# 28 of 48 modulation blocks computed on ScalarE and GpSimd instead of TensorE, in a two-layer diffusion backbone

## The chip, the cores and the metric

The kernel runs on one core of one Trainium2 chip. The metric is the device time of one execution in microseconds (us), the median over several runs. Engines are named as the profile names them: PE is TensorE, ACT is ScalarE, DVE is VectorE, POOL is GpSimd, SP is the engine that issues the DMAs.

## The reference, cut to what matters

Two layers over 256 latent and 256 context tokens of width 1024. Each layer turns a conditioning vector (`c` for latent tokens, `c_ctx` for context tokens) into six modulation vectors of 1024 numbers: shift, scale and gate of the mixer, and the same of the feed-forward.

```python
mod  = jax.nn.silu(c)     @ w_mod[l] + b_mod[l]      # w_mod[l]: 1024 x 6144
modc = jax.nn.silu(c_ctx) @ w_mod[l] + b_mod[l]
sh1, sc1, gt1, sh2, sc2, gt2 = jnp.split(mod[:, None, :], 6, axis=-1)
h = rms_norm(xl, g_pre_mix[l]) * (1.0 + sc1) + sh1
y, yc = token_mixer(h, hc, ...)          # conv branch, attention, pooling, merged by gates
xl = xl + gt1 * rms_norm(y, g_post_mix[l])
h = rms_norm(xl, g_pre_ffn[l]) * (1.0 + sc2) + sh2
xl = xl + gt2 * rms_norm(swiglu(h, ...), g_post_ffn[l])
```

The context tokens do the same with `modc`, in the first layer only (their second layer is never read).

## The kernel before

All products are float32, made of three passes of rounded floats: `split` (L345) writes `hi` on ACT (L347) and the rest `lo` on DVE (L348), and `mm3` (L328) multiplies hi·hi, hi·lo and lo·hi. Weights come in units of 128x1024, one DMA each, in the fixed order of `weight_order`; `unit` (L309) keeps about five units prepared ahead. A scheduler that goes by a simulated timeline then orders each engine's instructions and may move them past each other; on the chip each engine works its own list strictly in that order.

A layer (`layer`, L915) goes: V projection; eight heads, each with q and k projection (evicted at L606, one shuffled product on POOL at L611), scores, softmax (L704 to L716), transposes and the product with V (`head`, L719); in the first layer then the GLU projection (`glu`, L778) and the pooling projection, whose window sums run on POOL (`pool_group`, L876, L893 to L908); the depthwise convolution as 120 taps on DVE (L824) with a norm after it; `subln` (L748), which normalises the heads' outputs four heads at a time; three rounds of eight `merge` steps (attention, pooling, conv branch, in this order; L977); the output projection; the feed-forward's 22 pairs of units (L1089) and its output projection. The second layer does GLU and taps first.

The modulation is made in **blocks** of 256 columns: 24 per layer, four to each of the six vectors (`j` = 0 to 5; 2 and 5 are the gates). `mod_product` (L373) multiplies a block on PE: eight plain-float32 matmuls with 32 columns of `silu(c)` (`self.cc`, of which two are not zero), four chunks of the 1024 side by side in four strips of 32 rows. `mod_close` (L387) ends a block. For a shift or a scale ACT copies the strips out (L416), PE transposes them (L422, two), DVE adds the four strips, the bias and so on into `modv`. For a gate ACT and DVE split the strips, and PE spreads them over all partitions for each vector (`v`: latent, context) with two matmuls (L400, L401); DVE adds the bias and multiplies the norm's gain (L410, L412) into `G`, the tile that `residual` reads.

Eight blocks are made at the very start (shift and scale of layer 0's mixer). The others lie along the way: the mixer gate in the heads (L954), shift and scale of the feed-forward in the last merge round (`new_modv_fill`, L1106), four blocks at the end of the output projection `wo` (three in the second layer) and three at the end of `fo`, where PE would otherwise wait for the norm (L557, L585), and the rest beside the feed-forward's pairs (L1095). `BUFS` (L220) says how many buffers each kind of tile has: `mod` (a block's weights) has 2, `V` 18.

Of the kernel before, what the change touches and what calls it, by code (L numbers as in the profile page):

```python
# [30 lines left out]
DEPTH = 2  # L33
# [15 lines left out]
COL_G = 4608  # L49
UW = 1024  # L50


O_BM = 0
O_GM = 48
O_GF = 56
# [140 lines left out]
def lay_mod(w):  # L196

    m = w["w_mod"].reshape(DEPTH, 2, 4, P, 24, 256)
    return np.ascontiguousarray(m.transpose(0, 4, 1, 3, 2, 5)).reshape(
        DEPTH * 48, P, UW)  # L200


class Net:
    def __init__(self, ctx, tc, io):
# [14 lines left out]

    BUFS = {"raw": 4, "hi": 4, "lo": 4, "rawx": 4, "hix": 2, "lox": 3, "mod": 2, "H": 4, "V": 18, "O": 8, "Q": 10,  # L220
            "E": 7, "A": 6, "T": 4, "S": 2, "G": 4, "row": 2, "rows": 3, "sq": 4, "K2": 2, "QD": 1, "QH": 2, "QL": 2, "st": 25, "sh": 1,
# [165 lines left out]
    def mod_close(self, l, b, ps, gate=None):  # L387
# [46 lines left out]
        if j in (1, 4):  # L434
            nc.vector.scalar_tensor_tensor(out=d, in0=d, scalar=1.0,
                                           in1=col(O_GM if j == 1 else O_GF),
                                           op0=ALU.add, op1=ALU.mult)

    def new_modv(self, l):
# [103 lines left out]
    def out_proj(self, l, kind, nkp, acts, ntt, x, jg, tail, last, fill=()):  # L543
# [233 lines left out]

    def glu(self, l, acts, n, after_first):  # L778

        nc = self.nc  # L780
        us = []
        for i in range(NCC):
# [132 lines left out]
    def layer(self, l, H, acts, first, xin, xnext, tail):  # L915
# [12 lines left out]
        if not need_ctx:  # L928
            us = self.glu(l, acts, n, None)
            taps, norm = self.conv_tasks(l, us, nseq, ya)  # L930
            self.bg.extend(taps)
# [4 lines left out]
        pend = None  # L936
        self.new_G(l, 2)
        fill = deque(range(8, 12))
        for h in range(NH):
# [14 lines left out]
            if h % 2 == 0 and fill:  # L954
                self.mod_block(l, fill.popleft(), bank=self.H_BK)
        os.append(self.head(l, *pend, lam, need_ctx))

        if need_ctx:
            us = self.glu(l, acts, n, None)
            taps, norm = self.conv_tasks(l, us, nseq, ya)  # L960
        else:
            self.drain()
# [42 lines left out]
        for n_ in range(KC):  # L1005
            merge(1, n_, yb, ("ao", l, n_), 0)
            self.step(self.S_B)

# [19 lines left out]
        x = self.load_x(xin, ntt, "Q")  # L1028
        self.new_modv_fill(l)
        for n_ in range(KC):  # L1030
            merge(0, n_, ya, ("co", l, n_ // 2) if n_ % 2 == 0 else None,
                  (n_ % 2) * 4)
            if self.fill:
                self.fill.popleft()()
            if n_ >= 4 and self.fill:
                self.fill.popleft()()
        while self.fill:
            self.fill.popleft()()

# [49 lines left out]
        for i in range(i0, NFF):  # L1089
# [5 lines left out]
            if fill:  # L1095
                self.mod_block(*fill.popleft(), bank=self.FF_BK)
        while fill:
# [8 lines left out]
    def new_modv_fill(self, l):  # L1106

        self.fill = deque()
        for part in range(4):
            for j in (3, 4):  # L1110
                if l > 0 and (part, j) in ((0, 3), (0, 4), (1, 3)):
                    continue
                self.fill.append(lambda b=j * 4 + part: self.mod_block(l, b, bank=self.FL_BK))

# [10 lines left out]
    def run(self):  # L1125
        nc, io = self.nc, self.io
        self.prm, self.modv, self.G = {}, {}, {}
        self.perm = self.sb.tile([P, NPERM], F32, tag="perm", name="perm", bufs=1)
        const = self.perm[:, 0:C_TAB]
# [10 lines left out]
        self.ones512 = const[:, C_ONE:C_ONE + 1].to_broadcast([P, P])  # L1140
        perm_r = self.sb.tile([P, 6], F32R, tag="permr", name="perm_r", bufs=1)
# [4 lines left out]
        self.eps = self.perm[:, M_EPS:M_EPS + 1]  # L1146
        nc.vector.memset(self.eps, EPS)
        self.cc = (self.perm[:, M_CC:M_CC + 32 * KC]
# [130 lines left out]
```

## Time and profile before

| | |
|---|---|
| median of 3 runs | 1562.87 us (1561.74 to 1565.12) |
| the profiled execution | 1560.56 us, its span 1558.8 us |
| busy share of the span: PE, DVE, ACT, POOL | 98%, 63%, 48%, 9% |
| granted TensorE clock, mean | 0.995 of 2.4 GHz |
| DMA: moved, mean rate | 236.69 MB, 152 GB/s |

An engine's share is an average over stages. Matmuls are pipelined: in the records of a row of them each starts about 0.23 us (512 columns) or 0.12 us (256 columns) after the one before, though each is shown as lasting longer. So the cost of a matmul is read from start to start.

### The profile page before, as it was taken

The page shows a single profiled execution, that of the slowest core. Times are in us where ns is not written, and L with a number is a line of the kernel's source. Part 1 is how long each engine was busy: PE and PEld are TensorE (multiplying, and loading weights), DVE is VectorE, ACT ScalarE, POOL GpSimd, SP SyncE. Part 2 cuts the span into 40 slices and gives each one's busy share as a digit, 9 for nine tenths or more (in the row PEclk, how much of TensorE's full clock was granted, in tenths as well). Part 3 has the DMA queues.
Part 4 walks back from the last instruction along what each step waited for, and adds up shares of the span by engine and source line. Part 5 has one row for each costly group of instructions (what it writes and reads, how often), then busy time and mean ns, then how long its engine had stood idle before and what let it go on. Part 6 is the DMA issues. An engine that isn't in the chain of part 4 may idle for free.

```text
span 1558.8 us, 22462 instructions
## 1 busy us (share of the span) xinstructions
PE 1521.7 (98%) x8616; PEld 1254.0 (80%) x8616; DVE 979.8 (63%) x1626; ACT 740.6 (48%) x1254; POOL 144.5 (9%) x170
## 2 busy tenths in 40 slices
PE   6999999999999999999999999999998999999998
PEld 3778878878777688877888888888787799799986
DVE  4588786899964337434333222899999665665544
ACT  5467767432344236322222221836576565554443
POOL 0000100640131100000000000001012312100000
PEclk9999999999999999999999999999999999999999
DMA  9643343133335544456322234534344674546553
GB/s 347 200 121 95 108 136 95 69 117 100 128 111 193 201 143 149 145 169 202 102 95 95 95 122 162 201 126 135 107 133 146 245 257 167 208 157 206 185 191 108
DMA packets 81691, 236.69 MB, mean 152 GB/s; under 512 B 9648, under 2 KB 18480, under 8 KB 81584
## 3 DMA queue, kind: packets, MB, share of 16 engines
q1 hardware_dynamic: 81584, 235.26, 46.1%
q8 instruction: 67, 1.10, 0.3%
q14 instruction: 40, 0.33, 0.1%
HBM read 223.69 MB, written 5.24 MB: 147 GB/s over the span
## 4 chain that ended last, share of the span: by engine, by line
PE 89%; DVE 5%; ACT 2%; DMA 1%; issue 1%; POOL 1%; SPq 0%; DVEq 0%; ACTq 0%; POOLq 0%
PE psg L332 15%; PE psg L331 15%; PE psg L333 15%; PE pss L331 10%; PE pss L333 10%; PE pss L332 9%; PE pso L332 3%; PE pso L331 3%; PE pso L333 3%; PE pss L701 2%; PE pss L380 2%; PE pst L380 1%; PE pst L732 1%; DVE Q L824 1%; DVE lo L348 1%
## 5 line engine op out<-in xcount | busy, mean ns | idle before, releaser
L347 ACT ACTIVATE hi<-raw 128x1024 fp32r<-128x1024 f32 x299 | 314.7, 1055 | 523.0 <-issue 155.0
L348 DVE TENSOR_TENSOR lo<-raw,hi 128x1024 fp32r<-128x1024 f32 x299 | 373.3, 1250 | 278.3 <-ACT hi L347 273.7
L331 PE MATMUL psg<-H,hi 128*128 128x512 f32 (+1 forms) x864 | 299.8, 348 | 2.6 <-ACT E L707 1.5
L332 PE MATMUL psg<-H,hi 128*128 128x512 f32 (+1 forms) x864 | 299.2, 347 | 0.7 <-DVE H L348 0.7
L333 PE MATMUL psg<-H,lo 128*128 128x512 f32 (+1 forms) x864 | 299.7, 347 | 0.0
L331 PE MATMUL pss<-H,hi 128*128 128x256 f32 (+1 forms) x704 | 236.6, 337 | 1.8 <-ACT H L347 1.7
L333 PE MATMUL pss<-H,lo 128*128 128x256 f32 (+1 forms) x704 | 235.4, 335 | 0.0
L332 PE MATMUL pss<-H,hi 128*128 128x256 f32 (+1 forms) x704 | 234.4, 333 | 0.2 <-DVE H L348 0.2
L331 PEld LDWEIGHTS psg<-H,hi 128*128 128x128 f32 x864 | 162.1, 188 | 29.6 <-issue 3.2
L332 PEld LDWEIGHTS psg<-H,hi 128*128 128x128 f32 x864 | 162.3, 188 | 24.5 <-issue 3.4
L333 PEld LDWEIGHTS psg<-H,lo 128*128 128x128 f32 x864 | 162.4, 188 | 22.5 <-issue 2.2
L331 PEld LDWEIGHTS pss<-H,hi 128*128 128x128 f32 x704 | 132.5, 189 | 18.9 <-issue 2.5
L332 PEld LDWEIGHTS pss<-H,hi 128*128 128x128 f32 x704 | 133.8, 190 | 14.3 <-DVE H L348 0.4
L333 PEld LDWEIGHTS pss<-H,lo 128*128 128x128 f32 x704 | 132.6, 188 | 14.9
L611 POOL TENSOR_TENSOR sh<-sh,perm 128x256 f32<-128x256 f32 x32 | 27.8, 868 | 817.8 <-DMA raw<-w 494.2
L824 DVE SCALAR_TENSOR_TENSOR Q<-Q,perm,Q 128x482 f32<-128x482 f32 (+14 forms) x120 | 99.3, 827 | 2.5
L1070 DVE TENSOR_TENSOR S<-pss,S 128x256 f32<-128x256 f32 (+1 forms) x43 | 23.9, 555 | 80.0 <-PE pss L333 80.0
L707 ACT ACTIVATE E<-pss,st 128x512 f32<-128x512 f32 (+1 forms) x96 | 58.7, 614 | 31.9 <-DVE st L704 27.1
L331 PE MATMUL psg<-V,hi 128*128 128x512 f32 (+1 forms) x192 | 64.5, 341 | 1.8 <-ACT S L760 1.3
L332 PE MATMUL psg<-V,hi 128*128 128x512 f32 (+1 forms) x192 | 64.7, 338 | 0.8 <-DVE V L348 0.8
L333 PE MATMUL psg<-V,lo 128*128 128x512 f32 (+1 forms) x192 | 64.3, 336 | 0.0
L998 POOL TENSOR_TENSOR O<-O,S 128x512 f32<-128x512 f32 (+1 forms) x32 | 45.8, 1432 | 185.3 <-DVE S L996 166.4
(370 smaller groups left out, 2587.5 us busy)
## 6 DMA issues: line engine op xcount, KB each, us to landing
raw<-w SPq DMA_DIRECT2D x297, 512.0 KB, 3.4
mod<-wmod SPq DMA_DIRECT2D x66, 512.0 KB, 4.3
A<-wmod SPq DMA_DIRECT2D x18, 256.0 KB, 5.9
O<-wmod SPq DMA_DIRECT2D x16, 256.0 KB, 5.0
QD<-T SPq DMA_DIRECT2D x32, 128.0 KB, 2.4
E<-wmod SPq DMA_DIRECT2D x14, 256.0 KB, 5.3
row<-b_mod SPq DMA_DIRECT2D x24, 128.0 KB, 4.0
xs<-Q SPq DMA_DIRECT2D x12, 256.0 KB, 2.1
```

Source lines behind the costliest of these rows:

```text
L331: mm(out, sh, mh, start=start, stop=False)
L332: mm(out, sh, ml, start=False, stop=False)
L333: return mm(out, sl, mh, start=False, stop=stop)
L347: return (self.nc.scalar.activation(hi, src, AF.Copy), (lo_eng or self.nc.vector).tensor_tensor(out=lo, in0=src, in1=hi.bitcast(F32), op=A ...
L348: (lo_eng or self.nc.vector).tensor_tensor(out=lo, in0=src, in1=hi.bitcast(F32), op=ALU.subtract))
L380: ins = nc.tensor.matmul(ps[32 * kk:32 * kk + 32, 0:256], self.cc[:, k, :], raws[k], start=(k < 4), stop=(k >= 4), tile_position=(0, 32 * ...
L611: nc.gpsimd.tensor_tensor(out=sh, in0=sh, in1=self.sin, op=ALU.mult)
L701: nc.tensor.matmul(pss[j][:, :n], q[a][:, j, qt * P:(qt + 1) * P], k[:, j, k0:NT], start=(a == 0), stop=(a == 1))
L707: nc.scalar.activation(e[:, :n], pss[j][:, :n], AF.Exp, bias=mx[:, j:j + 1], accum_out=ss[:, j:j + 1])
L824: last[0] = nc.vector.scalar_tensor_tensor(out=av, in0=uv, scalar=prm[:, w:w + 1], in1=av, op0=ALU.mult, op1=ALU.add)
L998: nc.gpsimd.tensor_tensor(out=m[:, :n], in0=m[:, :n], in1=gs[:, :n], op=ALU.add)
L1070: nc.vector.tensor_tensor(out=s[:, :n], in0=pg[:, :n], in1=s[:, :n], op=ALU.mult)
```

## The change

Of the 48 blocks, 28 no longer go through PE's product. `WIDE` names them in pairs, as 14 **wide blocks** of 512 columns: eight of layer 0 (both gates, feed-forward shift and scale) and six of layer 1. All of them are worked during the first layer. A wide block comes as four DMAs of 128x1024, two chunks of 128 input rows each. For every chunk and vector ACT multiplies the weights by the chunk's `silu(c)`, one number per partition (AF.Copy with a scale, 128x512), and POOL adds the product to a running sum (`mt` holds products, `ma` sums, two buffers each). After the eighth chunk the sum is split (ACT, and POOL for `lo`), and `wide_close` adds over the partitions on PE: two matmuls of 512 columns with a matrix of ones per vector. A gate then gets its bias and gain from PSUM as before; a shift or scale is picked out of the spread rows with the identity on DVE. Context vectors are left out where the second layer doesn't need them.

The four parts of a wide block are handed out two per head, one per GLU step and merge step, and one per feed-forward pair or output step; the close is put off by one part. The blocks in the waits of `wo` and `fo` stay on PE; block 17 goes from the second layer's last merge round to its heads. `V` loses two buffers.

```diff
+WIDE = ((4, 5, 6, 7, 8, 9, 10, 11), (1, 3, 4, 5, 7, 9))
...
-    BUFS = {"raw": 4, ..., "mod": 2, "H": 4, "V": 18, "O": 8, "Q": 10,
+    BUFS = {"raw": 4, ..., "mod": 2, "mt": 2, "ma": 2, "H": 4, "V": 16, "O": 8, "Q": 10,
...
+        def part(q):
+            def f():
+                raw = self.t("mod", [P, UW])
+                dma = nc.sync.dma_start(out=raw, in_=self.io["wmod"][l * 48 + 4 * b + q])
+                self.after(self.last_dma, dma)
+                for kk in range(2):
+                    k = 2 * q + kk
+                    src = raw[:, kk * 512:(kk + 1) * 512]
+                    for v in range(nv):
+                        t = self.c2("mt" if k else "ma")
+                        nc.scalar.activation(t, src, AF.Copy, scale=self.cc[:, k, v:v + 1])
+                        if k == 0:
+                            accs[v] = t
+                        else:
+                            nc.gpsimd.tensor_tensor(out=accs[v], in0=accs[v], in1=t,
+                                                    op=ALU.add)
+                self.wide_late()
+                if q == 3:
+                    hl = {}
+                    for v, acc in accs.items():
+                        hl[v] = self.c2("sq", F32R), self.c2("sq", F32R)
+                        self.split(*hl[v], acc, nc.gpsimd)
+                    self.late = lambda: self.wide_close(l, b, hl)
...
+    def wide_close(self, l, b, hl):
...
+        for v, (hi, lo) in hl.items():
+            ps = self.ps("t")
+            one = self.one_r.to_broadcast([P, P])
+            nc.tensor.matmul(ps, one, hi, start=True, stop=False)
+            nc.tensor.matmul(ps, one, lo, start=False, stop=True)
...
-            if i == 0 and after_first is not None:
-                after_first()
+            self.wide(1)
...
-        self.new_G(l, 2)
-        fill = deque(range(8, 12))
+        if need_ctx:
+            self.new_G(l, 2)
+            self.wq.extend(t for b in WIDE[l][:6] for t in self.wide_tasks(l, b))
+        fill = deque() if need_ctx else deque([17])
...
+            self.wide(2)
...
-            todo = deque((l + 1, b + j) for b in range(4) for j in (0, 4)) + todo
+            todo = deque((l + 1, b + j) for b in range(2) for j in (0, 4))
...
+            for k in [(l, b) for b in WIDE[l][6:]] + [(l + 1, b) for b in WIDE[l + 1]]:
+                self.wq.extend(self.wide_tasks(*k))
```

Of the many rows that move, three places are shown, as each engine's list has them. Line numbers of the changed kernel are higher: L467 is the new product, L471 the new sum, L490 and L491 the close, and L341 to L343, L357, L358, L703, L804, L810, L842, L990, L996, L1001 and L1005 are what L331 to L333, L347, L348, L606, L707, L713, L745, L893, L899, L904 and L908 were.

PE in the feed-forward of layer 0, between two units; before, one gate block (L380) with the spreading of the block before it:

```order
L333 MATMUL pss_6156<-H_4929,lo_5972 128x512
L380 MATMUL pst_6228<-mod_6224,perm 32x256 x4
L380 MATMUL pst_6228<-mod_6226,perm 32x256
L400 MATMUL pst_6129<-rows_6138,perm_r 128x256
L401 MATMUL pst_6129<-rows_6138,perm_r 128x256
L380 MATMUL pst_6228<-mod_6226,perm 32x256 x3
L331 MATMUL pss_6254<-H_4928,hi_6001 128x512
```

Now, at the close of a wide gate block:

```order
L343 MATMUL pss_6366<-H_5115,lo_6196 128x512
L490 MATMUL pst_6446<-sq_6357,perm_r 128x512
L491 MATMUL pst_6446<-sq_6358,perm_r 128x512
L490 MATMUL pst_6455<-sq_6361,perm_r 128x512
L491 MATMUL pst_6455<-sq_6362,perm_r 128x512
L341 MATMUL pss_6464<-H_5114,hi_6225 128x512
```

A block's eight matmuls of 256 columns (x4 counts matmuls) and its four spreading ones, of which two stand here, give way to four of 512 columns that serve two blocks and both vectors.

ACT in the heads of layer 0, about the q eviction of the sixth head (`T`); before:

```order
L707 ACTIVATE E_1685,st_1676<-pss_1678,st_1677 128x256
L707 ACTIVATE E_1688,st_1676<-pss_1679,st_1677 128x256
L621 ACTIVATE K_1602<-T_1595 64x512 x2
L347 ACTIVATE hi_1566<-raw_1564 128x1024
L713 ACTIVATE E_1688<-E_1688,st_1690 128x256
L606 ACTIVATE T_1844<-psg_1819 128x512
L707 ACTIVATE E_1704,st_1695<-pss_1697,st_1696 128x256
L707 ACTIVATE E_1707,st_1695<-pss_1698,st_1696 128x256
L347 ACTIVATE A_1651<-pst_1646 128x512
L347 ACTIVATE A_1666<-pst_1661 128x512
```

Now:

```order
L804 ACTIVATE E_1769,st_1760<-pss_1762,st_1761 128x256
L357 ACTIVATE A_1750<-pst_1745 128x512
L467 ACTIVATE mt_1908<-mod_1897,perm 128x512
L804 ACTIVATE E_1772,st_1760<-pss_1763,st_1761 128x256
L467 ACTIVATE mt_2127<-mod_2125,perm 128x512
L357 ACTIVATE QH_1644<-QD_1639 128x1024
L804 ACTIVATE E_1788,st_1779<-pss_1781,st_1780 128x256
L718 ACTIVATE K_1686<-T_1679 64x512 x2
L810 ACTIVATE E_1772<-E_1772,st_1774 128x256
L467 ACTIVATE mt_2130<-mod_2125,perm 128x512
L357 ACTIVATE hi_1650<-raw_1648 128x1024
L703 ACTIVATE T_1942<-psg_1917 128x512
```

Three products of a wide block stand between the exponentials (L804), the weight splits and the eviction; up to the last GLU gate 72 products and eight splits of sums are added.

POOL at the end of the pooling branch of layer 0 (`A` tiles); before:

```order
L908 TENSOR_TENSOR A_3076<-A_3076,V_3077 128x256
L893 TENSOR_TENSOR A_3091<-A_3092 128x265
L893 TENSOR_TENSOR A_3092<-A_3091 128x257
L899 TENSOR_SCALAR A_3076<-A_3092 128x256
L904 TENSOR_TENSOR A_3076<-A_3092,perm 128x2x8
L908 TENSOR_TENSOR A_3076<-A_3076,V_3090 128x256
L831 TENSOR_TENSOR row_4017<-Q_3225,Q_3455 128x512
```

Now:

```order
L1001 TENSOR_TENSOR A_3328<-A_3331,perm 128x2x8
L990 TENSOR_TENSOR A_3344<-A_3343 128x269
L1005 TENSOR_TENSOR A_3328<-A_3328,V_3329 128x256
L471 TENSOR_TENSOR ma_3493<-ma_3493,mt_3582 128x512
L990 TENSOR_TENSOR A_3343<-A_3344 128x265
L471 TENSOR_TENSOR ma_3495<-ma_3495,mt_3585 128x512
L990 TENSOR_TENSOR A_3344<-A_3343 128x257
L471 TENSOR_TENSOR ma_3493<-ma_3493,mt_3588 128x512
L996 TENSOR_SCALAR A_3328<-A_3344 128x256
L471 TENSOR_TENSOR ma_3495<-ma_3495,mt_3591 128x512
L1001 TENSOR_TENSOR A_3328<-A_3344,perm 128x2x8
L1005 TENSOR_TENSOR A_3328<-A_3328,V_3342 128x256
```

Four sums stand among the last window sums; from the first row of the pooling branch to its last there are nine instructions of wide blocks. On ACT the conversion of that last `A` tile still stands ahead of the conversion of the last heads' outputs, and PE's list has 31 more matmuls between the last pooling projection and the first use of the seventh head's output than it had.

## Rows read from the trace of the kernel before

**Rows 1.** The page: busy time (share) and instructions; then the chain by engine.
```profile
PE 1521.7 (98%) x8616; PEld 1254.0 (80%) x8616; DVE 979.8 (63%) x1626; ACT 740.6 (48%) x1254; POOL 144.5 (9%) x170
...
PE 89%; DVE 5%; ACT 2%; DMA 1%; issue 1%; POOL 1%; SPq 0%; DVEq 0%; ACTq 0%; POOLq 0%
```

**Rows 2.** Windows: stretch, length, busy us (instructions) of PE, PEld, DVE, ACT, POOL; clock; DMA.
```profile
68.40:280.00 211.60, 209.79 (x1071) 168.92 (x1070) 166.66 (x336) 147.22 (x288) 13.12 (x20) 1.00 0.39 115
280.00:340.00 60.00, 58.58 (x265) 44.85 (x264) 57.10 (x65) 25.43 (x40) 41.10 (x56) 1.00 0.25 84
1000.00:1100.00 100.00, 100.00 (x576) 86.14 (x575) 92.40 (x185) 57.30 (x100) 7.83 (x8) 1.00 0.40 127
1100.00:1200.00 100.00, 94.70 (x620) 80.09 (x620) 94.81 (x193) 64.69 (x123) 10.14 (x20) 0.98 0.47 148
1200.00:1220.00 20.00, 15.15 (x97) 9.06 (x99) 12.95 (x25) 10.79 (x22) 13.85 (x21) 0.83 0.30 105
```

**Rows 3.** Timeline of PE at one block's product: start us, us, then the instruction.
```profile
400.57 0.39 PE L331 MATMUL psg<-E,hi 128*128 128x512 f32 x1
400.89 1.07 PE L380 MATMUL pss<-mod,perm 128*32 128x256 f32 x16
401.89 0.50 PE L331 MATMUL psg<-H,hi 128*128 128x512 f32 x1
402.23 0.39 PE L332 MATMUL psg<-H,hi 128*128 128x512 f32 x1
```

**Rows 4.** Timeline of PE at one block's two transposes.
```profile
493.96 0.39 PE L333 MATMUL psg<-H,lo 128*128 128x512 f32 x1
494.19 0.38 PE L422 MATMUL pss<-perm,rows 128*128 128x128 f32 x2
494.33 0.48 PE L331 MATMUL psg<-H,hi 128*128 128x512 f32 x1
494.65 0.40 PE L332 MATMUL psg<-H,hi 128*128 128x512 f32 x1
```

**Rows 5.** Timeline of PE where one vector of a gate block is spread.
```profile
234.48 0.28 PE L400 MATMUL pst<-rows,perm_r 128*128 128x256 f32 x1
...
234.72 0.40 PE L333 MATMUL psg<-H,lo 128*128 128x512 f32 x1
```

**Rows 6.** Groups by shape: busy us, mean ns, idle before, for ACT, POOL and DVE.
```profile
L713 ACT ACTIVATE E<-E,st 128x512 f32<-128x512 f32 x32 | 23.1, 721 | 12.6 <-DVE st L712 12.4
...
L998 POOL TENSOR_TENSOR O<-O,S 128x512 f32<-128x512 f32 x16 | 25.1, 1568 | 112.5 <-DVE S L996 96.8 <-DVE perm L426 15.7
...
L611 POOL TENSOR_TENSOR sh<-sh,perm 128x256 f32<-128x256 f32 x32 | 27.8, 868 | 817.8 <-DMA raw<-w 494.2 <-DVE sh L608 245.2 <-DVE st L711 29.3
...
L609 DVE TENSOR_TENSOR T<-T,perm 128x256 f32<-128x256 f32 x32 | 17.9, 559 | 0.2
...
L412 DVE TENSOR_TENSOR G<-G,row 128x256 f32<-128x256 f32 x24 | 10.1, 420 | 0.2
```

**Rows 7.** Timelines of DVE and POOL: two taps, one of them beside a GpSimd add.
```profile
429.02 0.72 DVE L824 SCALAR_TENSOR_TENSOR Q<-Q,perm,Q 128x494 f32<-128x494 f32 x1
...
429.78 1.65 DVE L824 SCALAR_TENSOR_TENSOR Q<-Q,perm,Q 128x492 f32<-128x492 f32 x1
...
429.19 1.71 POOL L998 TENSOR_TENSOR O<-O,S 128x512 f32<-128x512 f32 x1 [5.33 <-DVE S L996]
```

**Rows 8.** Timelines of POOL, ACT and PE around the end of the pooling branch.
```profile
286.80 2.23 POOL L893 TENSOR_TENSOR A<-V 128x271 f32<-128x271 f32 x1 [3.73 <-ACT V L888]
...
327.86 0.73 POOL L908 TENSOR_TENSOR A<-A,V 128x256 f32<-128x256 f32 x1
...
328.62 0.63 ACT L347 ACTIVATE E<-A 128x512 fp32r<-128x512 f32 x1 [0.53 <-POOL A L908]
...
331.53 0.50 PE L332 MATMUL psg<-V,hi 128*128 128x512 f32 x1 [0.78 <-DVE V L348]
```

**Rows 9.** Timeline of PE at a block in the second layer.
```profile
1205.76 1.92 PE L380 MATMUL pss<-mod,perm 128*32 128x256 f32 x16
```

More of the change, by code (lines that the diff above doesn't have):

```diff
@@ L198, in lay_mod @@
     m = w["w_mod"].reshape(DEPTH, 2, 4, P, 24, 256)
-    return np.ascontiguousarray(m.transpose(0, 4, 1, 3, 2, 5)).reshape(
-        DEPTH * 48, P, UW)
+    m = np.ascontiguousarray(m.transpose(0, 4, 1, 3, 2, 5)).reshape(DEPTH * 48, P, UW)
+    for l in range(DEPTH):
+        for b in WIDE[l]:
+            q = w["w_mod"][l][:, b * 512:b * 512 + 512].reshape(4, 2, P, 512)
+            m[l * 48 + 4 * b:l * 48 + 4 * b + 4] = q.transpose(0, 2, 1, 3).reshape(4, P, UW)
+    return m
 class Net:
@@ L437, in mod_close, with wide_tasks @@
                                            op0=ALU.add, op1=ALU.mult)
+    def wide_tasks(self, l, b):
+        nc = self.nc
+        nv = 2 if l < DEPTH - 1 or b < 4 else 1
+        accs = {}
+        def part(q):
[21 more added lines that the diff above has]
+                    self.late = lambda: self.wide_close(l, b, hl)
+            return f
+        return [part(q) for q in range(4)]
@@ new lines, in wide_close, with colof @@
+    def wide_close(self, l, b, hl):
+        nc = self.nc
+        j, half = b // 2, b % 2
+        for v, (hi, lo) in hl.items():
[3 more added lines that the diff above has]
+            nc.tensor.matmul(ps, one, lo, start=False, stop=True)
+            if j in (2, 5):
+                G = self.G[l, j, v]
+                col = slice(half * 512, half * 512 + 512)
+                post = "g_post_mix" if j == 2 else "g_post_ffn"
+                for src, op in ((self.io["b_mod"][l:l + 1, j * D + col.start:j * D + col.stop],
+                                 ALU.add), (self.io[post][l:l + 1, col], ALU.mult)):
+                    rb = self.t("row", [P, 512])
+                    nc.sync.dma_start(out=rb, in_=src.to_broadcast([P, 512]))
+                    nc.vector.tensor_tensor(out=G[:, col], in0=ps if op == ALU.add else G[:, col],
+                                            in1=rb, op=op)
+                continue
+            pv = ps.rearrange("p (c t) -> p c t", c=4)
+            nc.vector.tensor_tensor(out=pv, in0=pv,
+                                    in1=self.ident.unsqueeze(1).to_broadcast([P, 4, P]),
+                                    op=ALU.mult)
+            d = self.modv[l, j][:, 4 * half:4 * half + 4, v]
+            nc.vector.tensor_reduce(out=d, in_=pv, axis=AX.X, op=ALU.add)
+            prm = self.prm[l]
+            def colof(o):
+                return prm[:, o + 4 * half:o + 4 * half + 4]
+            nc.vector.tensor_tensor(out=d, in0=d, in1=colof(O_BM + j * 8), op=ALU.add)
+            if j in (1, 4):
+                nc.vector.scalar_tensor_tensor(out=d, in0=d, scalar=1.0,
+                                               in1=colof(O_GM if j == 1 else O_GF),
+                                               op0=ALU.add, op1=ALU.mult)
@@ L439, in new_modv, with wide, wide_late @@
+    def wide(self, n):
+        while n > 0 and self.wq:
+            self.wq.popleft()()
+            n -= 1
+        if not self.wq and n > 0:
+            self.wide_late()
+    def wide_late(self):
+        late, self.late = self.late, None
+        if late is not None:
+            late()
     def new_modv(self, l):
@@ L791, in glu @@
             us.append(u)
-            if i == 0 and after_first is not None:
-                after_first()
+            self.wide(1)
         return us
@@ L1006, in layer @@
             merge(1, n_, yb, ("ao", l, n_), 0)
+            self.wide(1)
             self.step(self.S_B)
@@ L1096, in layer @@
                 self.mod_block(*fill.popleft(), bank=self.FF_BK)
+            if i >= 4:
+                self.wide(1)
         while fill:
@@ L1104, in layer @@
                       ahead)
[L1106 to L1113, printed above, removed]
     def load_x(self, src, ntt, tag):
@@ L1146, in run @@
         self.eps = self.perm[:, M_EPS:M_EPS + 1]
+        nc.vector.memset(self.eps, 1.0)
+        nc.vector.tensor_copy(self.one_r, self.eps)
         nc.vector.memset(self.eps, EPS)
```

22 lines of the change are left out of this document (10 added, 12 removed).

## The prediction

> **What bounds the kernel now.** I read the page first. PE is busy for 98% of the span and makes up 89% of the chain that ended last [rows 1], so work that leaves PE is worth its own length wherever PE waits for nobody, and nothing where it waits. The second view, the windows, tells the two apart [rows 2]. From 68.4 to 280 us, the heads and the GLU of layer 0, PE is full, but DVE is busy for 166.7 and ACT for 147.2 of 211.6 us: those are the engines that the change loads. From 280 to 340 us DVE is at 95% and POOL at 41.1 of 60 us. In layer 1, DVE at 92.4% still leaves PE full; at 94.8% PE loses 5 of 100 us; and from 1200 to 1220 us PE is busy for 15.2 of 20 us, at a mean granted clock of 0.83, between its two levels of 1.2 and 2.4 GHz, because it waits. The third view, the timeline of PE, gives prices from start to start.
>
> **What leaves PE.** A block's product: from the matmul before it to the second after it 1.66 us pass, of which two ordinary matmuls would take 0.46: 1.20 us [rows 3]. Two transposes: 0.69 less 0.46, 0.23 us [rows 4]. Spreading one vector of a gate block: 0.24 us [rows 5]. By the plan, 4 blocks leave the heads of layer 0, 8 its merges, 8 its feed-forward, and 8 layer 1 (three in the heads, since block 17 comes in for four gate blocks, and five in the merges). That is 28 products, 33.6 us; 16 pairs of transposes, 3.7; and 20 spreadings (8 gate blocks with two vectors, 4 with one), 4.8: **42.1 us off**.
>
> **What comes to PE.** Ten wide blocks with two vectors and four with one make 48 matmuls of 512 columns, at 0.23 us: **11.0 us on**. They go in a row, so nothing is added for a change of kind. Net 31.1 us.
>
> **Where that can't be had.** Two of layer 1's blocks lie between 1200 and 1220 us. The first shows 1.92 us, drawn out, since PE had nothing else [rows 9]; taking it away leaves PE waiting for the same chain. I count both, 1.43 us each with their transposes, at nothing, so 28.2 us remain. The bound below is nothing lost, above also a longer time at the half clock; a few us at most in a stretch of 20.
>
> **What ACT gets.** By its order, 72 products and eight splits of sums fall between the first q eviction and the last GLU gate of layer 0. A scaled copy of 128x512 takes 0.72 us [rows 6], so 80 take 57.7 us. 147.2 + 57.7 = 205 us, in a stretch where PE now needs 211.6 less 4 x 1.20 and 8 x 0.24 plus four closes of 0.92, 208.6 us. ACT would be 98% full, with its waits in between. The trace has no such stretch on ACT. If all gaps close the cost is nothing; if ACT keeps the share that it has there now (70%) the stretch grows by 84 us. The nearest rows are the full DVE of layer 1, 92.4% with PE full and 94.8% with PE losing [rows 2]. At their mean, 93.6%, the stretch takes 219 us: **10 us lost**, which is what I take. Of the rest, two wide blocks fall into layer 0's merges and the others beside its feed-forward, where ACT is mostly idle; there they cost nothing.
>
> **What POOL gets, and through it DVE.** A sum of 128x512 takes 1.57 us on average [rows 6]; 80 instructions in the heads and GLU make 126 us, which fit beside the 13.1 there now. But POOL and DVE slow each other. A DVE product of 256 columns that always has POOL's L611, 868 ns, beside it (L609) takes 559 ns where a like one takes 420; a tap beside a sum of 1.71 us takes 1.65 us where its neighbour takes 0.72 [rows 6, 7]. So DVE loses between 16% and 54% of POOL's time, 20 to 68 us here; I take a quarter, 32, since much of what DVE reads there is PSUM. DVE then has 199 of 208.6 us, 95%, a little less than ACT: covered by the 10 us.
>
> The Trainium skill, SBUF — State Buffer, section "Who interferes with whom", says that a DVE instruction with two SBUF inputs contends with a GpSimd instruction that reads SBUF, and that the port pair is locked so that the loser fully blocks. The two pairs above agree that there is contention, but DVE lost 0.14 us of a POOL instruction's 0.87 and 0.93 of another's 1.71, not the whole; what the whole would cost is the last rival.
>
> **The pooling branch.** Its window sums keep POOL at work from 286.8 to 328.6 us; the last one's conversion on ACT follows at once, and the last heads' outputs behind it in ACT's list; PE waits 0.78 us there already [rows 8]. Now nine wide instructions stand inside that chain: 9 x 1.57 = 14.1 us later. PE's list has 31 more matmuls ahead of the place, 7.1 us. I take the rest, **7 us lost**; the bounds are 0 and 14. The taps end later by POOL's contention too, but a wait of PE in front of them gives them that time.
>
> Free of cost: the first products before 68 us, in ACT's gaps; the four one-vector closes at the end of layer 0's `fo`, where PE waits for the norm; the wide DMAs, of the same bytes, each queued behind a weight unit, with five units prepared ahead; and two buffers less of `V`. Should SP stall on a `mod` buffer for longer than four units last (24 matmuls of 0.23 us each, 22 us together), that cover is gone; ACT frees a buffer after four products.
>
> **Sum.** -42.1 + 11.0 + 2.9 + 10 + 7 = -11.2 us. Against the profiled execution of 1560.56 us that is 1549.4; it stood 2.3 us below the median of 1562.87, so I forecast **1552 us**, 1543 to 1558 if this case holds.
>
> **Rivals.** A measurement of this kernel can tell about 0.2%, 3.1 us, from no change.
>
> *All is hidden.* ACT's products only fill its gaps and the schedule's extra matmuls cover the pooling branch. For it: every added instruction is of a kind with long slack, and DVE at 92.4% left PE full. Against it: 98% on ACT. Time: 1563 - 31 = 1532, within 3.
>
> *DVE pays more.* Half-way between its two prices, 35% of POOL's time, DVE loses 44 us in the heads: 211 of 208.6, at 93.6% a stretch of 225, 17 us longer, and the pooling branch its whole 14: 28.2 - 31 leaves +3, 1566; with the 7 us, 1559. So about 1562, no change.
>
> *ACT is held by POOL (slower).* The product tiles have two buffers, and ACT works strictly in order. Four products take ACT 2.9 us and POOL 6.3, so a part whose products stand close holds ACT for up to 3.4 us, and behind it stand the exponentials, evictions and splits that PE needs. For 18 parts in the heads: 61 us if nothing stands between, half if, as in the order, one or two others do. ACT then has 236 to 266 us, the stretch grows by 27 to 57, and the time is 1569 to 1599, in the middle 1584. It decides from 1.4 us a part, where 205 + 18 x 1.4 exceeds 208.6 by the 21 us that are left to lose. For it: sums are slower than products two to one. Against it: the average distance of products, 2.6 us, is more than a sum.
>
> *DVE is locked out whole (slower).* If each of the 80 POOL instructions cost DVE its full length, DVE had 167 + 126 = 293 us in the heads, 84 more than PE; with 14 in the pooling branch the time is 1563 - 28 + 98 = 1633. This is what the rule of the Trainium skill above comes to; the rows of the two pairs [rows 6, 7] speak against it.
>
> **Chances.** Forecast 0.43; all hidden 0.22; DVE pays more 0.15; ACT held 0.16; DVE locked out 0.02; the rest 0.02. Faster by over 0.2% (below 1559.7) takes the first two, 0.06 of the third and 0.01 of the rest: 0.72; within 0.2%: 0.09 of the third and 0.01 of the rest, 0.10; slower: the two slower rivals, 0.18. The range from 1530 to 1571 leaves out a part of "all hidden" and most of "ACT held", some 0.18.
>
> **What would show it.** PE's product at 16 records [rows 3] for each of 20 blocks, not 48; heads and GLU of layer 0 some 7 us longer with ACT at 93 to 95%; a wait of PE at the first use of the last heads' outputs; merges and feed-forward of layer 0 shorter by 10 and 7 us; layer 1 by some 9. Wrong, if the heads are no longer than before (all hidden), if ACT's idle time there ends on POOL (the slower rival), or if DVE's L348 and taps are longer by over a third.

## The result, and the profile after

The changed kernel takes **1635.91 us** (median of 4 runs, 1632.23 to 1637.40) beside 1562.30 of the kernel before on the same chip: a ratio of 1.0471, with a 95% interval of 1.0458 to 1.0484. It is 4.7% slower. The forecast was 1552, and the range, up to 1571, did not hold it. The profiled execution has a span of 1630.5 us.

The page of the changed kernel, busy time and the chain that ended last:

```profile
PE 1520.0 (93%) x8144; PEld 1261.0 (77%) x8144; DVE 1058.5 (65%) x1605; ACT 866.2 (53%) x1444; POOL 422.0 (26%) x362
...
PE 71%; DVE 14%; ACT 6%; DMA 4%; issue 3%; POOL 1%; SPq 1%; DVEq 0%; ACTq 0%; POOLq 0%
```

PE has 472 instructions less than in [rows 1], and hardly less busy time, because more of it runs at half clock: 67 us of that time lie where 1.2 GHz was granted, against 13 before. Its share of the chain falls from 89 to 71%. To see where, I cut both traces at the same instructions:

| stage | before, us | after | change | forecast |
|---|---|---|---|---|
| to the first q eviction | 68.4 | 69.1 | +0.7 | 0 |
| heads and GLU of layer 0 | 211.7 | 243.5 | +31.8 | +7 |
| pooling, merges, `wo`, to the first SiLU of the feed-forward | 342.3 | 349.7 | +7.4 | -3 |
| feed-forward | 243.5 | 233.8 | -9.7 | -7 |
| `fo`, to the first GLU sigmoid of layer 1 | 141.3 | 191.4 | +50.1 | 0 |
| layer 1 | 551.6 | 543.0 | -8.6 | -9 |

Of the 84 us above the forecast 50 lie in `fo`, 25 in heads and GLU, and 10 from the pooling branch to `wo`.

The windows of the changed kernel, columns as in [rows 2]: the heads, the feed-forward, `fo`, and what follows `fo`:

```profile
69.10:312.60 243.50, 221.59 (x1027) 173.43 (x1026) 210.33 (x330) 191.79 (x363) 121.62 (x94) 0.96 0.39 124
...
662.30:896.10 233.80, 233.80 (x1028) 189.25 (x1028) 101.91 (x107) 116.95 (x163) 96.41 (x67) 1.00 0.43 151
896.10:1018.00 121.90, 121.90 (x572) 100.15 (x574) 38.74 (x49) 34.56 (x52) 0.00 (x0) 1.00 0.43 144
1018.00:1068.00 50.00, 11.10 (x38) 6.12 (x30) 11.62 (x26) 23.66 (x40) 36.99 (x29) 0.54 0.59 198
```

Two things stand out. GpSimd does nothing at all in `fo`, 122 us long, and then works for 37 of 50 us in which PE has next to nothing and its clock is granted at 0.54. And the heads are longer although no engine is full there: DVE 210.3 of 243.5 us, 86%; ACT 191.8, 79%.

**After `fo`.** The timelines of SP, PE and POOL of the changed kernel; the last column is the idle time before, and what ended it:

```profile
880.78 0.42 SPq L460 DMA_DIRECT2D mod<-wmod  x1
881.25 5.82 SPq L369 DMA_DIRECT2D mod<-wmod  x2
887.17 71.45 SPq L305 DMA_DIRECT2D raw<-w  x14
...
1015.63 1.07 PE L390 MATMUL pso<-mod,perm 128*32 128x256 f32 x16
...
1016.33 0.80 SPq L460 DMA_DIRECT2D mod<-wmod  x2
...
1022.33 6.52 POOL L471 TENSOR_TENSOR ma<-ma,mt 128x512 f32<-128x512 f32 x5 [132.48 <-ACT mt L467]
...
1028.33 0.79 PE L490 MATMUL pst<-sq,perm_r 128*128 128x512 f32 x1 [8.97 <-ACT sq L357]
```

At 881 SP begins to load block 12 of layer 1 into the two `mod` buffers (L369); the second load starts at 887. This block is meant for the wait at the end of `fo`, and PE uses it at 1015.6. Until then both buffers are taken, no wide part can load (L460), and the 14 that were handed out beside `fo` run one after the other behind it; PE's list has their closes ahead of the norm's transposes. The profile of PE's waits gives four waits for such a sum (the split `sq` that L490 multiplies) 34.0 us, the longest 9.1:

```profile
PE pst L490 <- ACT sq L357: 34.0, 4, 9.1
```

**In the heads.** Timelines of POOL, DVE, ACT and PE of the changed kernel at one place of the softmax:

```profile
109.88 4.59 POOL L471 TENSOR_TENSOR ma<-ma,mt 128x512 f32<-128x512 f32 x3
...
112.00 1.33 DVE L709 TENSOR_TENSOR T<-T,sh 128x256 f32<-128x256 f32 x1
113.25 0.15 DVE L808 RECIPROCAL st<-st 128x2 f32<-128x2 f32 x1
113.44 1.05 DVE L809 TENSOR_TENSOR st<-st,perm 128x1 f32<-128x1 f32 x1
...
114.58 0.51 ACT L810 ACTIVATE E<-E,st 128x256 f32<-128x256 f32 x1 [2.21 <-DVE st L809]
114.99 1.04 ACT L357 ACTIVATE hi<-raw 128x1024 fp32r<-128x1024 f32 x1
115.94 0.46 ACT L804 ACTIVATE E<-pss,st 128x256 f32<-128x256 f32 x1
...
116.54 0.50 PE L798 MATMUL pss<-K,QH 128*128 128x512 f32 x1 [2.56 <-ACT E L804]
```

A product of one column on DVE (L809), 0.15 us long by itself, lasts 1.05: it ends at 114.49, just after the third sum, at 114.47. ACT waits 2.21 us for it, the next exponential stands behind in ACT's list, and PE waits 2.56 us for the PSUM tile that this exponential frees. Not all of ACT's wait is this one product: L709 ahead of it, 0.42 us long by itself, was drawn out to 1.33 by the second sum in the same way, and a weight split of 1.04 us (L357) stands in ACT's list before the exponential. Over the whole stretch, the largest of PE's waits, ACT's wait for a buffer of the products, and the sums:

```profile
PE pss L798 <- ACT E L804: 11.9, 9, 2.6
...
ACT mt L467 <- POOL ma L471: 4.6, 5, 1.7
...
L471 POOL TENSOR_TENSOR ma<-ma,mt 128x512 f32<-128x512 f32 x65 | 96.4, 1499 | 50.6 <-ACT mt L467 45.3 <-ACT ma L467 5.1
```

### The profile page after: what moved, and what is told of

It reads as the page before. It is cut to its first block, busy times and chain, and to the rows that moved or that the text cites. A ratio compares the mean times of both kernels' runs of the same rounds, so it can differ in the third digit from the quotient of the medians.

```text
span 1630.5 us, 21988 instructions
## 1 busy us (share of the span) xinstructions
PE 1520.0 (93%) x8144; PEld 1261.0 (77%) x8144; DVE 1058.5 (65%) x1605; ACT 866.2 (53%) x1444; POOL 422.0 (26%) x362
## 3 DMA queue, kind: packets, MB, share of 16 engines
q8 instruction: 64, 1.05, 0.3%
## 4 chain that ended last, share of the span: by engine, by line
PE 71%; DVE 14%; ACT 6%; DMA 4%; issue 3%; POOL 1%; SPq 1%; DVEq 0%; ACTq 0%; POOLq 0%
PE psg L341 11%; PE psg L342 11%; PE psg L343 11%; PE pss L343 9%; PE pss L342 9%; PE pss L341 9%; DMA mod<-wmod 2%; PE pso L342 2%; PE pso L343 2%; PE pso L341 2%; DVE lo L358 2%; DVE Q L921 2%; DVE st L801 1%; DVE O L921 1%; DVE K L719 1%
## 5 line engine op out<-in xcount | busy, mean ns | idle before, releaser
L358 DVE TENSOR_TENSOR lo<-raw,hi 128x1024 fp32r<-128x1024 f32 x299 | 386.2, 1294 | 293.3 <-ACT hi L357 271.2
L357 ACT ACTIVATE hi<-raw 128x1024 fp32r<-128x1024 f32 x299 | 314.2, 1055 | 442.8 <-PE psg L342 147.3
L471 POOL TENSOR_TENSOR ma<-ma,mt 128x512 f32<-128x512 f32 x168 | 245.0, 1477 | 474.4 <-ACT mt L467 467.5
L341 PE MATMUL psg<-H,hi 128*128 128x512 f32 (+1 forms) x864 | 302.7, 352 | 5.1 <-ACT H L357 2.8
L343 PE MATMUL psg<-H,lo 128*128 128x512 f32 (+1 forms) x864 | 303.3, 352 | 0.0
L342 PE MATMUL psg<-H,hi 128*128 128x512 f32 (+1 forms) x864 | 302.8, 351 | 0.3 <-DVE H L358 0.3
L343 PE MATMUL pss<-H,lo 128*128 128x256 f32 (+1 forms) x704 | 236.8, 337 | 0.0
L341 PE MATMUL pss<-H,hi 128*128 128x256 f32 (+1 forms) x704 | 234.4, 334 | 0.1
L341 PEld LDWEIGHTS psg<-H,hi 128*128 128x128 f32 x864 | 165.3, 192 | 29.6 <-ACT H L357 3.7
L342 PEld LDWEIGHTS psg<-H,hi 128*128 128x128 f32 x864 | 165.6, 192 | 24.4 <-issue 1.9
L343 PEld LDWEIGHTS psg<-H,lo 128*128 128x128 f32 x864 | 165.3, 191 | 23.9 <-issue 2.0
L341 PEld LDWEIGHTS pss<-H,hi 128*128 128x128 f32 x704 | 132.7, 189 | 15.4 <-ACT H L357 0.8
L343 PEld LDWEIGHTS pss<-H,lo 128*128 128x128 f32 x704 | 132.6, 188 | 13.8
L467 ACT ACTIVATE mt<-mod,perm 128x512 f32<-128x512 f32 x168 | 113.0, 713 | 39.2 <-DMA mod<-wmod 34.4
L921 DVE SCALAR_TENSOR_TENSOR Q<-Q,perm,Q 128x482 f32<-128x482 f32 (+14 forms) x120 | 108.3, 903 | 2.1
L804 ACT ACTIVATE E<-pss,st 128x512 f32<-128x512 f32 (+1 forms) x96 | 58.5, 611 | 25.2 <-DVE st L801 16.9
L343 PE MATMUL psg<-V,lo 128*128 128x512 f32 (+1 forms) x192 | 66.0, 345 | 1.6 <-DVE lo L358 1.6
```

The costliest lines, as they stand in the source:

```text
L341: mm(out, sh, mh, start=start, stop=False)
L342: mm(out, sh, ml, start=False, stop=False)
L343: return mm(out, sl, mh, start=False, stop=stop)
L357: return (self.nc.scalar.activation(hi, src, AF.Copy), (lo_eng or self.nc.vector).tensor_tensor(out=lo, in0=src, in1=hi.bitcast(F32), op=A ...
L358: (lo_eng or self.nc.vector).tensor_tensor(out=lo, in0=src, in1=hi.bitcast(F32), op=ALU.subtract))
L467: nc.scalar.activation(t, src, AF.Copy, scale=self.cc[:, k, v:v + 1])
```

## The experiments

All times are medians; the ratio is to the kernel before on the same chip, with its 95% interval. The last columns say how many us later than before, in the profiled executions, the GLU of layer 0 ends (its last sigmoid), the feed-forward of layer 0 begins, and the GLU of layer 1 begins.

| run | us | ratio | GLU 0 | FFN 0 | GLU 1 |
|---|---|---|---|---|---|
| the changed kernel | 1635.91 | 1.0471 (1.0458 to 1.0484) | +32.5 | +39.9 | +80.4 |
| fo_buffers | 1587.78 | 1.0167 (1.0152 to 1.0182) | +32.8 | +41.3 | +33.6 |
| heads_on_PE | 1593.95 | 1.0209 (1.0194 to 1.0224) | -1.5 | -1.4 | +38.2 |
| both_undone | 1546.51 | 0.9905 (0.9888 to 0.9921) | -1.5 | -1.4 | -9.1 |
| small_sums | 1602.36 | 1.0264 (1.0248 to 1.0280) | +11.9 | +8.5 | +49.1 |
| small_products | 1630.22 | 1.0442 (1.0428 to 1.0456) | +30.3 | +38.2 | +77.1 |
| split_sums | 1634.34 | 1.0465 (1.0449 to 1.0481) | +21.4 | +38.4 | +81.0 |
| wide_in_merges | 1556.60 | 0.9968 (0.9958 to 0.9979) | +0.6 | +12.4 | +4.7 |
| dve_in_merges | 1551.44 | 0.9938 (0.9925 to 0.9950) | -0.7 | +5.6 | -2.1 |
| both_undone_again | 1544.68 | 0.9891 (0.9873 to 0.9910) | -1.0 | -1.0 | -8.7 |
| dve_late | 1535.30 | 0.9830 (0.9813 to 0.9847) | -1.5 | -10.7 | -16.9 |
| more_beside_ffn | 1546.00 | 0.9893 (0.9873 to 0.9912) | +0.1 | -0.2 | -4.7 |
| late_and_more | 1537.95 | 0.9844 (0.9826 to 0.9861) | +2.2 | -6.8 | -14.4 |

**fo_buffers**

```diff
-            ahead = [((l + 1, 12), None), ((l + 1, 16), "OOOO"), ...]
+            ahead = [((l + 1, 12), "VVVV"), ((l + 1, 16), "OOOO"), ...]
```

> The block whose load is issued at the start of layer 0's fo takes its weights in four V tiles instead of the two mod tiles; nothing else is changed. Theory A (held buffers): in the changed kernel that load keeps both mod tiles from the first unit of fo until the block is multiplied at fo's end, so the 14 wide parts that belong beside fo all run after it; fo's end came 50 us later against before than the feed-forward's end did. With the tiles free those parts run beside fo's matmuls and the time falls by 40 to 50 us, to 1586 to 1596 us, with no wait of PE for the sums at the close. Rival B (the sums themselves are too slow: 14 parts are 98 instructions of GpSimd and as many products): they drag on beside fo as well, slow its weight splits, and less than 20 us comes back, 1616 us or more.

It came out as theory A says: 48.1 us less, all of it between the beginning of the feed-forward (+41.3 here, +39.9 in the changed kernel) and layer 1 (+33.6 and +80.4). Rival B's count was wrong besides: the 14 parts are not 98 instructions of GpSimd but the 29 that stand in the last window above. Windows of this run, `fo` and the 40 us behind it:

```profile
900.00:1020.00 120.00, 120.00 (x537) 99.03 (x536) 44.21 (x63) 52.20 (x82) 35.10 (x27) 1.00 0.61 216
1020.00:1060.00 40.00, 38.73 (x309) 34.76 (x309) 34.55 (x74) 26.76 (x55) 0.00 (x0) 1.00 0.43 144
```

The sums now run beside `fo`'s matmuls, PE stays full and at full clock, and nothing is left behind it.

**heads_on_PE and both_undone**

```diff
-WIDE = ((4, 5, 6, 7, 8, 9, 10, 11), (1, 3, 4, 5, 7, 9))
+WIDE = ((10, 11), (1, 3, 4, 5, 7, 9))
...
-        fill = deque() if need_ctx else deque([17])
+        fill = deque(range(8, 12)) if need_ctx else deque([17])
...
+        if need_ctx:
+            self.new_modv_fill(l)
```

> The six wide blocks of layer 0's heads, GLU and merges go back to TensorE as before the change; the eight wide blocks beside the feed-forward stay wide, fo's load as it is in the changed kernel. Theory C (the heads' wide work costs more than it saves): the 39 us that the changed kernel is behind at the end of layer 0's merges are gone, feed-forward (-9 us), fo (+50 us) and layer 1 (-9 us) stay: 1595 us, 1590 to 1600. Rival D (the delay is moved, not made, there: PE would wait for the same work elsewhere): less than half comes back, 1616 us or more.

> Both edits together: heads and merges on TensorE, fo's load in V tiles, eight wide blocks beside feed-forward and fo. If A and C hold and add up, what is left is the gain of the feed-forward and of layer 1: 1563 - 9 - 9 = 1545 us, 1541 to 1552, faster than before. If the wide parts beside fo cost what they save (B), 1555 to 1575 us.

Both hold. The two losses are separate and add up: 48.1 and 42.0 us back one by one, 89.4 together. What remains of the change, eight wide blocks beside feed-forward and `fo`, is a gain: 1546.51 us.

**small_sums and small_products**

In small_sums:

```diff
+    w = 16 if l == 0 and b < 10 else 512
-    nc.gpsimd.tensor_tensor(out=accs[v], in0=accs[v], in1=t, op=ALU.add)
+    nc.gpsimd.tensor_tensor(out=accs[v][:, :w], in0=accs[v][:, :w], in1=t[:, :w], op=ALU.add)
```

In small_products:

```diff
+    w = 16 if l == 0 and b < 10 and k else 512
-    nc.scalar.activation(t, src, AF.Copy, scale=self.cc[:, k, v:v + 1])
+    nc.scalar.activation(t[:, :w], src[:, :w], AF.Copy, scale=self.cc[:, k, v:v + 1])
...
+    nc.gpsimd.tensor_tensor(out=accs[v][:, w:], in0=accs[v][:, w:], in1=src[:, w:], op=ALU.add)
```

> The sums of the six wide blocks of layer 0's heads and merges add 16 columns instead of 512 (the other columns of these modulation vectors lack seven of their eight chunks); the products on ACT stay whole. Theory E (GpSimd's sums slow DVE, and the softmax chain with it): the GLU of layer 0 ends 0 to 10 us after that of before instead of 32, DVE's weight split is back near 1.22 us from 1.48; 1600 to 1612 us. Rival F (ACT's products, standing between the exponentials in ACT's list, delay the softmax): it still ends 20 us or more after, 1622 to 1636 us.

> The other half of the heads' load taken away: ACT's products of the six wide blocks of layer 0's heads and merges are 16 columns instead of 512 after the first chunk, and GpSimd adds the raw weights in the other 496 columns, in a second instruction (so these modulation vectors are sums of unweighted rows). Theory E (in the lock between GpSimd's sums and those DVE instructions that read two SBUF tiles lies the larger part): GLU of layer 0 still ends 17 us or more after that of before, 1618 to 1632 us. Rival F (only products and sums together lose time, ACT's 58 us being the main part): 12 us or less, 1604 to 1615 us.

Without the sums' width 33.6 us come back; without the products' width 5.7. So the sums carry the larger part of the loss in heads and merges and the products little, though not nothing: with small sums GLU still ends 11.9 us late, a little above what theory E allowed. The two are not a sum of parts (11.9 and 30.3 against 32.5), perhaps since a product that is late matters only where the softmax is already late; that was not shown. Nor is small_products the pure opposite: GpSimd makes two instructions of each sum there and is busy for 145.8 us instead of 121.6, so 5.7 us may be too little. The scheduler orders each of these kernels anew, so single microseconds should not be read from them.

The DVE instructions in the heads, grouped by shape: before, changed, small_sums (L810 and L707 there are L809 and L706 of the changed kernel, L712 and L609 of before; the maxima are L704, L801 and L802):

```profile
L609 DVE TENSOR_TENSOR T<-T,perm 128x256 f32<-128x256 f32 x16 | 10.1, 631 | 0.1
L712 DVE TENSOR_TENSOR st<-st,perm 128x1 f32<-128x1 f32 x32 | 6.5, 203 | 0.2
L704 DVE TENSOR_REDUCE st<-pss 128x1 f32<-128x512 f32 x32 | 21.3, 680 | 4.5 <-PE pss L701 4.4
```

```profile
L706 DVE TENSOR_TENSOR T<-T,perm 128x256 f32<-128x256 f32 x16 | 14.8, 923 | 0.3
L808 DVE RECIPROCAL st<-st 128x2 f32<-128x2 f32 x32 | 5.0, 157 | 4.3 <-ACT E L804 3.9
L809 DVE TENSOR_TENSOR st<-st,perm 128x1 f32<-128x1 f32 x32 | 12.9, 403 | 0.3
L801 DVE TENSOR_REDUCE st<-pss 128x1 f32<-128x512 f32 x32 | 21.2, 675 | 0.0
```

```profile
L707 DVE TENSOR_TENSOR T<-T,perm 128x256 f32<-128x256 f32 x16 | 8.4, 524 | 0.4
L810 DVE TENSOR_TENSOR st<-st,perm 128x1 f32<-128x1 f32 x32 | 4.8, 151 | 0.2
L802 DVE TENSOR_REDUCE st<-pss 128x1 f32<-128x512 f32 x32 | 21.3, 677 | 0.0
```

Here a form is one instruction of the code at one shape. Forms with two SBUF inputs are longer in the changed kernel and short again with small sums; the maximum over a PSUM tile is the same everywhere. Taking each form's records without a GpSimd instruction beside them as its own length, the records with one are longer by 50.6 us in all over the changed kernel's heads, by 5.0 before, and by 5.6 in small_sums.

**split_sums**

```diff
-    nc.gpsimd.tensor_tensor(out=accs[v], in0=accs[v], in1=t, op=ALU.add)
+    w = 128 if l == 0 and b < 10 else 512
+    for c in range(0, 512, w):
+        nc.gpsimd.tensor_tensor(out=accs[v][:, c:c + w], in0=accs[v][:, c:c + w],
+                                in1=t[:, c:c + w], op=ALU.add)
```

> Each sum of layer 0's heads and merges in four GpSimd instructions of 128 columns instead of one of 512; nothing left out. Theory E1 (a DVE instruction with two SBUF inputs waits until the GpSimd instruction that is running has ended; in the changed kernel the one-column product in the softmax, 149 ns alone, takes 828 ns on average under a sum): waits shrink with the instruction, the one-column product falls to 250 ns or less on average under a sum, and GLU ends 8 us or more earlier than in the changed kernel, below 1628 us. Rival E2 (the two share a bandwidth, so DVE pays a share of GpSimd's busy time whatever its pieces): DVE loses as much or more than now, 1636 us or more.

Half right. DVE behaves as E1 says: the time lost to GpSimd falls from 50.6 to 22.5 us although GpSimd is busy for 175.8 us there instead of 121.6, which E2 does not allow, and GLU ends 11 us earlier. But the time does not move. The groups in the heads of this run:

```profile
L473 POOL TENSOR_TENSOR ma<-ma,mt 128x128 f32<-128x128 f32 x252 | 152.0, 638 | 27.0 <-ACT mt L467 23.8 <-ACT ma L467 3.1
...
L812 DVE TENSOR_TENSOR st<-st,perm 128x1 f32<-128x1 f32 x30 | 9.1, 302 | 0.2
```

Four pieces take 2.55 us, where one sum took 1.50; the one-column product falls to 302 ns only, and to 393 over the 19 that had a GpSimd instruction beside them, not the 250 expected (two of them waited for the next piece too); and ACT's waits for a product buffer grow from 4.6 to 14.3 us. The 11 us are gone again where the merges begin, 32.7 us late, and the pooling branch's last conversion on ACT comes 66 us later than before, where the changed kernel has 45; which of these took them was not tried apart.

**wide_in_merges, dve_in_merges, dve_late.** Can the eight blocks of the feed-forward's shift and scale leave PE later, where the taps end?

In wide_in_merges, beside both_undone:

```diff
-WIDE = ((10, 11), ...)
+WIDE = ((6, 7, 8, 9, 10, 11), ...)
...
             merge(2, n_, yc, ...)
+            self.wide(1)
...
             merge(0, n_, ya, ...)
+            self.wide(1)
```

In dve_in_merges and dve_late also, for these four blocks' chunks from the second on (their `lo` moves from GpSimd to DVE as well; dve_late has no part after `merge(2, ...)` and two after `merge(0, ...)`):

```diff
+    nc.vector.scalar_tensor_tensor(out=accs[v], in0=src, scalar=self.cc[:, k, v:v + 1],
+                                   in1=accs[v], op0=ALU.mult, op1=ALU.add)
```

> As both_undone, and the four wide blocks of layer 0's feed-forward shift and scale are worked in the last two merge rounds, where DVE's taps end, instead of eight blocks on TensorE. Those blocks' products and transposes are 8 x 1.43 us on PE, four closes of 0.92 us come in: 7.8 us. Theory H (there DVE and ACT have the slack): 1539 us, 1536 to 1542. Rival I (the lock: the sums meet the merges' own DVE work and the last taps): 1546 us or more.

> As wide_in_merges, but DVE makes product and sum of these four blocks in one instruction (scalar_tensor_tensor of 128x512, 0.75 us, 56 of them) and GpSimd nothing. Theory H: 1539 us, as wide_in_merges. Rival I says that without GpSimd's sums it is faster than wide_in_merges by 3 us or more. A third way, J (42 us more on DVE are too many beside the taps' end): slower than wide_in_merges by 3 us or more.

> As dve_in_merges (four wide blocks as 56 DVE instructions of 0.75 us), but all in the last merge round, after the conv branch's norm; dve_in_merges had PE wait 10 us for that norm's output and 3.4 us for its sums. Theory K (what was lost there was the chain of taps and norm, which the added work stood in): the wait is gone and the 7.8 us come in, 1538 to 1541 us. Rival L (in the last round the merges' own DVE work and the weight splits suffer as much): 1546 us or more.

Theory H fell: both are slower than both_undone, by 10 and 5 us (12 and 7 beside both_undone_again, which ran on their chip). Rival I holds in that GpSimd's sums cost there: without them dve_in_merges is 5.2 us faster. J, slower by 3 or more, fell. What PE waits for, in wide_in_merges from 390 to 640 us and in dve_in_merges:

```profile
PE pso L934 <- POOL row L931: 4.9, 1, 4.9
PE pst L491 <- POOL sq L358: 4.0, 3, 2.2
PE pst L490 <- ACT sq L357: 3.7, 3, 2.1
```

```profile
PE psg L341 <- ACT E L357: 10.0, 1, 10.0
PE pso L956 <- POOL row L953: 3.4, 1, 3.4
```

The longest wait is for the conv branch: in wide_in_merges for the sums of its norm, in dve_in_merges for its output after the norm. The added work stood in that chain. both_undone has neither wait there. dve_late starts the work one round later, as theory K would have it, and its window from 460 to 560 shows DVE nearly full with PE full:

```profile
460.00:560.00 100.00, 100.00 (x433) 81.15 (x433) 94.75 (x127) 45.36 (x62) 18.46 (x10) 1.00 0.66 221
```

PE has no wait for the conv branch left. At **1535.30 us** it is the fastest version: 1.7% below the kernel before, some 6% below the change as made. K holds, though its range of 1538 to 1541, reckoned from 1546.5, was missed by 3 us on the good side: beside both_undone_again on the same chip 9.4 us come in for the 7.8 of the sum.

**both_undone_again, more_beside_ffn, late_and_more**

```diff
-WIDE = (..., (1, 3, 4, 5, 7, 9))
+WIDE = (..., (0, 1, 2, 3, 4, 5, 7, 9))
...
-        fill = todo
+        fill = deque() if need_ctx else todo
...
-            if i >= 4:
-                self.wide(1)
+            self.wide(1)
```

> The kernel of both_undone once more, on the chip of the three kernels below, to compare them with: 1545 to 1548 us.

> As both_undone, and the four blocks of layer 1's mixer shift and scale that were still made on TensorE beside the feed-forward are two more wide blocks there, handed out from the second unit pair on. 4 x 1.43 us less two closes of 0.92: 3.9 us on PE. Theory M (beside feed-forward and fo nothing that PE waits for is touched): 1541 to 1544 us. Rival B (the sums, now 40 parts in 350 us, run behind the end of fo): 1548 us or more.

> dve_late and more_beside_ffn together. If K and M hold: 1546 - 7.8 - 3.9 = 1535 us, 1533 to 1538; if only M holds, 1542 us or more.

both_undone_again came out 0.3 us below its range. The other two are a miss by my reading of the code. The four blocks were not beside the feed-forward: in both_undone no block's product stands from 600 to 860 us, and four stand at the end of `wo`, from 593 to 598, where PE would otherwise wait for the norm. They stayed there, and the run made them a second time as wide blocks; it shows only that eight more parts and two closes beside feed-forward and `fo` cost 1 to 3 us. late_and_more lies in its range by luck: dve_late is better than its sum, and the 3.9 us of theory M did not come in.

## Why the prediction was wrong, point by point

- **"Free of cost: ... the four one-vector closes at the end of layer 0's `fo`, where PE waits for the norm; the wide DMAs"** is the step that failed most: 50.1 us instead of nothing, 48.1 of them given back by fo_buffers. The text named the right resource, a `mod` buffer that is not free, but took "ACT frees a buffer after four products" for the only user. The load that `out_proj` issues at its start holds the one for 134 us and the other for 129. It was to be seen in the list of ACT, where 28 products stand together behind `fo`'s last splits, and in the place of the closes in PE's list.
- **"What ACT gets": 10 us lost** in the heads was 35 by the same count (31.8 longer, with 3 us less on PE). The sum asked how full an engine is. ACT came to 79 and DVE to 86%, less than the 93.6% at which I let PE lose; PE lost through waits, 21.9 us idle, 11.9 of them in nine waits for an exponential, and through a clock granted at 0.96 on the mean. The products in ACT's list are the smaller part of it, as far as small_sums and small_products tell.
- **"What POOL gets, and through it DVE": a quarter of GpSimd's time** was too low. The surplus is 50.6 us less the 5.0 of before, 45.6 us where 32 were taken. Of the 108.5 us that GpSimd has more there (121.6 less 13.1) that is 42%, between the bounds of 16 and 54%; in us it is beside the 44 of the rival "DVE pays more". The misreading was of [rows 7]. I read that the tap lost 0.93 us of a sum of 1.71, so not the whole. But the tap began when 1.12 us of the sum were left, and ended 0.53 us after it: it waited for the sum's end. Nor does L609 always have L611 beside it, as the prediction says: in the heads before, nine of its sixteen begin inside L611, and each of these ends 280 to 286 ns after L611's end, however much of it was left (0.25 to 0.68 us), so that the mean of 559 ns hid the rule. The Trainium skill, SBUF — State Buffer, section "Who interferes with whom", says just this, that the loser fully blocks, and which instructions it concerns, two SBUF inputs on DVE; I set it aside by rows that agree with it.
- **The rival "DVE is locked out whole", 1633 us,** is near the measured time for a wrong sum. It charges DVE the full length of every GpSimd instruction, which is more than the rule that the prediction takes from the Trainium skill. It has the heads longer by 84 us less what PE saves, and they were longer by 32: a DVE instruction from PSUM does not pay, and one with two SBUF inputs pays the rest of the running sum, not all of it. The other 50 us were in `fo`.
- **The rival "ACT is held by POOL"** fell: in the heads ACT's products waited 4.6 us for a buffer of the sums, not 30 to 61.
- **The pooling branch and the merges:** -3 forecast, +7.4 measured. The 7 us were to be one wait for the last heads' outputs. The waits on their way come to 4.3 us, of 8.1 that PE is idle from the first to the eighth merge step; before, it was 1.4. The same steps before and after:

```profile
311.90:382.50 70.60, 69.18 (x294) 53.85 (x293) 69.44 (x85) 21.16 (x27) 17.73 (x20) 1.00 0.33 110
```

```profile
347.60:428.00 80.40, 72.31 (x289) 55.50 (x288) 79.43 (x91) 29.28 (x40) 40.23 (x32) 0.94 0.34 118
```

  DVE is full in both (98 and 99%): the steps are longer by 9.8 us, as its work is by 10.0. small_sums, which has the merges' sums small too, gives -3.4 (from +11.9 to +8.5), so what was lost hangs on the sums. The taps, which read two SBUF tiles, are longer beside GpSimd by 17 us in the changed kernel from the end of GLU on, by 8 before and in small_sums; that this is the whole of it was not shown.
- **What held:** blocks off PE pay their price where PE is full. Feed-forward -9.7 for 7, layer 1 -8.6 for 9, and the same lock costs PE nothing there: beside the feed-forward DVE's part of the weight split takes 1361 ns instead of 1225, on a DVE that is idle for over half of the time, while PE is full. Before and after:

```profile
L348 DVE TENSOR_TENSOR lo<-raw,hi 128x1024 fp32r<-128x1024 f32 x43 | 52.7, 1225 | 78.0 <-ACT hi L347 75.4 <-DMA raw<-w 0.2
```

```profile
L358 DVE TENSOR_TENSOR lo<-raw,hi 128x1024 fp32r<-128x1024 f32 x43 | 58.5, 1361 | 70.2 <-ACT hi L357 68.1
```

## What to carry to other kernels

Before work is called free because it hides beside a stage, list every user of the buffers that it loads through, and look for one that takes them early and uses them late; the new work starts when that one is done. Ask of an added load not only how full its engine gets but in whose chain it stands: a one-column instruction in the softmax was held for up to 1.1 us by a neighbour's sum. And a row that shows a partial loss is to be read at its end, against the end of the instruction beside it, before it is taken as a share.

## What the runs showed of the hardware

- In the heads of the changed kernel the one-column product L809 began twelve times inside a GpSimd instruction, and ended 13 to 21 ns after that instruction's end each time, whether 0.3 or 1.2 us of it were left. The 256-column products L706 and L709 ended 280 to 287 ns after it each time. The reciprocal L808 and the maxima from PSUM, beside the same sums, kept their length (157 and 675 ns). DVE's part of the weight split (L358, 1024 columns) ended 1079 to 1087 ns after it thirteen times; three that began with under 0.1 us of it left kept their length. So each that was held waited for the end and then took its own length (149, some 420, 1219 ns) less about 0.13 us. One more began within a nanosecond of a GpSimd instruction (at 285.54): there DVE kept its 1.22 us and GpSimd took 2.37. It is a lock that lasts for one instruction, by the order of starting.
- GpSimd pays in such company too: a sum of 128x512 takes 1.50 us on average in the heads (1.27 to 2.28), and 1.30 (five in 6.52 us) after `fo`, where DVE does next to nothing.
- After `fo`, with PE busy for 11.1 of 50 us, the clock was granted at 0.54 on the mean, between the two levels of 1.2 and 2.4 GHz; in fo_buffers, where PE did not stop, it stayed at 1.00.
